# The opening of a feed-forward up stage: sums, casts, a split, a gate and the next stage's first splits issued later; second halves' gates behind the next sums

## The chip, the cores and the metric

The kernel runs on one core of one Trainium2 chip. The metric is device time in microseconds (us) of one execution; a lower time is better. The core's engines work side by side, each on a queue of its own that it works off in order: TensorE (PE, matmuls), VectorE (DVE), ScalarE (ACT), GpSimd (POOL) and SyncE (SP, which here issues the DMAs). PEld is TensorE's weight load.

## The reference, cut to what matters

One decoder layer over 16 + 1024 tokens of width 1024. The first part mixes attention and a recurrence; the change touches its last blocks and what follows, which is the feed-forward part:

```python
h = h + rmsnorm(mix, ln_mix_post[l])
a = rmsnorm(h, ln_ffn_pre[l])
u = a @ w_up                       # 1024 x 5632, D_FF = 2816
u = causal depthwise conv of width 3 over tokens(u) + conv_b
gate, up = split(u, 2)
y = (gelu(gate) * up) @ w_down     # 2816 x 1024
h = h + rmsnorm(y, ln_ffn_post[l])
```

Every matmul is done in float32 accuracy: each operand is split into a rounded high part and a low remainder, and three products (high·high, high·low, low·high) replace one.

## The kernel before, in words

**Blocks.** The first part works in token blocks of 128. Its last step for a block (`post_a`, `post_b`) makes the residual `xh`, then the normalized activations `a2s`; `trans` turns these on TensorE (tile `pa`, L1112) and ACT copies them into `at2_0` or `at2_1`, one tile for each half p of the tokens (p = 0, 1; 512 tokens each). TensorE's order near 650 us is: the last output blocks, `trans(6)`, the first products of the up stage, with `trans(7)` and `trans(8)` between them.

**Up stage.** The 2816 gate columns and the 2816 up columns go in 22 units of 128 + 128 columns, ft = 0 to 21. A unit's weights come by DMA as four raw pieces `ra` (`load_raw4`, on SP, five buffers), GpSimd forms their sums `ws` (`w_sum`), ACT casts the high part `uh`, and DVE or GpSimd subtracts for the low part `ul` (`prep(q)`, q = 7·ft + j). The preparation for unit ft + 1 runs during unit ft.

Units 0 and 1 are `plain_unit`s: for each half, four column pieces of 24 matmuls into banks `pq`, each followed by an ACT copy into `ug` or `uu`. Units 2 to 21 are `unit`s: seven products j = 0 to 6 instead of eight (Winograd's form of Strassen), 12 matmuls each for each half, the halves taking turns. Products 0 and 4 go to bank `pa`, 1, 3 and 5 to `pb`, 2 and 6 to `pc`. Between products the engines read the banks: ACT copies `x1` out of `pa` after product 0; DVE makes `u2` = pb + x1 after product 1, and only then may product 3 write `pb` on; DVE makes `u3` after product 3, and only then product 5 may; then come the halves of `uu` and `ug`. Names end in unit and half: `u2_2_1` is u2 of unit 2, half 1.

The products' token operands are quarters of `at2` and their differences. `t_sums(p)` makes the differences in place (four subtractions of 128 x 1024, `at<-at` in the profile, and a small one for p = 0); `t_split(p, j)` splits a quarter into high (ACT cast) and low (DVE): tiles `t0_j`, `t1_j`. Unit 0 and 1 need j = 0, 4, 7, 6 of the plain quarters, the later units also 1, 2, 3, 5 of the sums.

**Gate.** `gated` takes a unit's `ug` and `uu`: an ACT step and two DVE steps for the convolution of each (tiles `c0` and `c1`), a gelu on ACT, the product on GpSimd (L1280) and a store by SP into `gsc` (L1281). The columns that a second half needs of the first are copied by ACT.

**Down stage.** It reads `gsc` back (`gi`), splits it (`gh` cast on ACT, `gl` on DVE), and multiplies. `ahead(i)` does this for step i, `LOOK` steps before it.

**Who sets the order.** TensorE's order is the written one. For the other engines a scheduler orders the instructions, and `with behind(names)` holds what is issued inside it on an engine's queue behind the instruction last noted in `marks[name]` on that engine; it makes no wait of its own across engines. `issue_after(marks["store"])` does the same on SP for the weight loads: they stand behind the noted store. DVE and ACT instructions go through a recording helper, so that nearly all of them carry line 53 in the profile; tiles tell them apart.

Of the kernel before, what the change touches and what calls it, by code (L numbers as in the profile page):

```python
# [13 lines left out]
ALU = mybir.AluOpType  # L14
# [10 lines left out]
NF = DFF // P  # L25
# [6 lines left out]
HALF = 256  # L32
# [53 lines left out]
def layer_kernel(ctx: ExitStack, tc: tile.TileContext, x, meta, table, lbl, gpre, gpost, win,  # L86
# [63 lines left out]
    def ps_s(name):  # L150
        return pp.tile([P, 2, 512], F32, tag="S", name=name)
# [912 lines left out]
    @contextmanager  # L1064
    def behind(*names):
        with ExitStack() as st:
            for nm in names:
                st.enter_context(tc.issue_after(marks[nm].ins))
            yield
# [68 lines left out]
                      7: (0, e + HALF, e + 2 * HALF), 6: (4, e + HALF, e + 2 * HALF)}[j]  # L1138
        return at2[p][:, k0:k0 + 4, c0:c1]

    def t_sums(p):
        b11, b12, b21, b22 = (quarter(p, j, False) for j in (0, 7, 4, 6))
        V.tensor_tensor(b11, b12, b11, op=ALU.subtract)
        V.tensor_tensor(b12, b22, b12, op=ALU.subtract)
        V.tensor_tensor(b22, b22, b11, op=ALU.subtract)
        V.tensor_tensor(b21, b21, b22, op=ALU.subtract)
        if EDGE[p]:
            e1, e2 = (at2[p][:, k0:k0 + 4, :EDGE[p]] for k0 in (0, 4))
            V.tensor_tensor(e2, e2, e1, op=ALU.subtract)

    def sum_quarter(p, j):
        return {1: lambda: quarter(p, 6), 2: lambda: quarter(p, 0, False), 3: lambda: quarter(p, 7), 5: lambda: quarter(p, 4)}[j]()
# [56 lines left out]
    for n, i in enumerate(order):  # L1209
        py = ps_s(f"py1_{i}")[:, 0]  # L1210
        before = order[n - 1] if n else None
        if i > 2:
            for _ in out_last(i):
                pass
        if i < 2:
            m = (m0, kept)[i]
            todo = [(m[:, 0, a:a + 2], m[:, 1, a:a + 2], a, a + 2, tok(i)[0]) for a in range(0, KD, 2)]
        else:
            todo = ms + [pre_last[i]]
        nxt = []  # L1220
        for c, part in enumerate(todo):
            if c == 2:
                if n == 0:
                    for p in range(3, NBLK):
                        pre_last[p] = mix_split(p, 7, 8)
                else:
                    post_b(before)
                    if n + 1 < NBLK:
                        x_in(order[n + 1])
            if c == 3 and n >= 2:  # L1230
                trans(order[n - 2])
            for _ in out_part(part, py, wo, c == 0, part is todo[-1]):
                pass
            if 1 < i < NBLK - 1 and c < 4:
                nxt.append(mix_load(i + 1, c))
        if i > 1:
            ms = nxt
        if i == 5:
            t_split(0, 0, quarter(0, 0), ep, "e0")
            t_split(0, 4, quarter(0, 4), ep, "e1")  # L1240
        if i == 6:
            t_split(0, 7, quarter(0, 7), mxp, "mix0", 272)
            t_split(0, 6, quarter(0, 6), mxp, "mix1", 384)
        if i == 7:
            t_sums(0)
        if i == 3:
            prep_plain(1, ("12", "22"))
        post_a(i, py)
    post_b(8)
    with behind("rstd"):  # L1250
        prep_plain(1, ("11", "21"))
    close(q_cm, kp_cm, ml_cm, w1_cm, y_cm)

    xu_cm, xup = pool("xu", 2)
# [6 lines left out]

    last = {}

    def conv(ft, p, side, u):
        m = ft + NF * side
        w = 2 * HALF
        if p:
            A.copy(u[:, :2], last[side][:, w:])
        last[side] = u
        c = cv.tile([P, w], F32, tag=f"c{side}", name=f"c{side}_{ft}_{p}", bufs=2 if side else 3)  # L1270
        A.activation(c, u[:, 2:2 + w], AF.Identity, bias=cbt[:, m:m + 1], scale=cwt[:, m, 2:3])
        V.scalar_tensor_tensor(c, u[:, 1:1 + w], cwt[:, m, 1:2], c, ALU.mult, ALU.add)
        V.scalar_tensor_tensor(c, u[:, 0:w], cwt[:, m, 0:1], c, ALU.mult, ALU.add)
        return c

    def gated(ft, p, ug, uu):
        cg = conv(ft, p, 0, ug)
        A.activation(cg, cg, AF.Gelu_apprx_tanh)
        cu = conv(ft, p, 1, uu)
        G.tensor_tensor(cg, cg, cu, op=ALU.mult)  # L1280
        st = SY.dma_start(gsc[P * ft: P * (ft + 1), 2 * HALF * p:2 * HALF * (p + 1)], cg)  # L1281
        if ft == p == 0:
            marks["store"] = st

    def plain_unit(ft, p, bank):
        us = outputs(ft, p)
        e = EDGE[p]
        for col in range(2):
            a, n = ((2 - e, HALF + e), (2 + HALF, HALF))[col]
            for side in range(2):  # L1290
                pt = bank(f"pq{ft}_{p}_{col}{side}")[:, :n]
                for kh in range(2):
                    hi, lo = plain[ft, f"{side + 1}{kh + 1}"]
                    th, tl = tt[p][(0, 4, 7, 6)[2 * col + kh]]
                    for k in range(4):
                        s = slice(P * k, P * (k + 1))
                        T.matmul(pt, hi[:, s], th[:, k], start=(kh + k == 0), stop=False)
                        T.matmul(pt, hi[:, s], tl[:, k], start=False, stop=False)
                        T.matmul(pt, lo[:, s], th[:, k], start=False, stop=(kh == 1 and k == 3))
                A.copy(us[side][:, a:a + n], pt)  # L1300
                yield
        with behind("turned"):
            gated(ft, p, *us)
        yield

    def unit(ft, p, bank):
        nm = f"{ft}_{p}"
        ug, uu = outputs(ft, p)
        e = EDGE[p]
        x1 = xup.tile([P, HALF + 2], F32, tag="x1", name=f"x1_{nm}")[:, 2 - e:]  # L1310
        u2, u3 = (xup.tile([P, HALF], F32, tag=t, name=f"{t}_{nm}") for t in ("u2", "u3"))

        def mm(j, pt, first):
            hi, lo = made[7 * ft + j]
            th, tl = tt[p][j]
            pt = pt[:, HALF + e - width(p, j):]
            for k in range(4):
                s = slice(P * k, P * (k + 1))
                T.matmul(pt, hi[:, s], th[:, k], start=(first and k == 0), stop=False, skip_group_check=True)  # L1319
                T.matmul(pt, hi[:, s], tl[:, k], start=False, stop=False, skip_group_check=True)  # L1320
                T.matmul(pt, lo[:, s], th[:, k], start=False, stop=(k == 3), skip_group_check=True)  # L1321

        pa = bank(f"pa{nm}")[:, :HALF + e]
        mm(0, pa, True)
        A.copy(x1, pa)
        yield
        pb = bank(f"pb{nm}")[:, :HALF + e]
        mm(1, pb, True)
        V.tensor_tensor(u2, pb[:, e:], x1[:, e:], op=ALU.add)
        yield  # L1330
        pc = bank(f"pc{nm}")[:, :HALF + e]
        mm(2, pc, True)
        yield
        mm(3, pb, False)
        V.tensor_tensor(u3, pb[:, e:], x1[:, e:], op=ALU.add)
        V.tensor_tensor(uu[:, 2 + HALF:], pc[:, e:], u3, op=ALU.add)
        yield
        mm(4, pa, False)
        A.copy(ug[:, 2 - e:2 + HALF], pa)
        yield  # L1340
        mm(5, pb, False)
        V.tensor_tensor(uu[:, 2 - e:2 + HALF], pb, x1, op=ALU.add)
        yield
        mm(6, pc, False)
        V.tensor_tensor(ug[:, 2 + HALF:], pc[:, e:], u2, op=ALU.add)
        gated(ft, p, ug, uu)
        yield

    free = [ps_in("pq0"), ps_in("pq1")]
    both = ps_s("pq2")  # L1350
    free += [both[:, 0], both[:, 1]]
    p0 = plain_unit(0, 0, lambda nm: free.pop(0))
    next(p0)
    with behind("xh"):
# [5 lines left out]
        t_split(1, 4, quarter(1, 4), tp, "t1_4")  # L1360
    next(p0)
    trans(8)
    t_split(1, 7, quarter(1, 7), tp, "t1_5")
    t_split(1, 6, quarter(1, 6), mxp, "mix2", 384)
    next(p0)
    with behind("hi", "lo"):
        t_split(0, 1, sum_quarter(0, 1), tp, "t0_1", 264)
        t_split(0, 2, sum_quarter(0, 2), tp, "t0_2")
        t_split(0, 3, sum_quarter(0, 3), tp, "t0_3")
# [8 lines left out]
        next(p1)  # L1378
    prep(14)
    prep(15)  # L1380
    t_sums(1)
    p0 = plain_unit(1, 0, ps_b)
    for j in range(4):
        next(p0)
# [8 lines left out]
    for j in range(4):  # L1393
        next(p1)
    prep(17)
    t_split(1, 5, sum_quarter(1, 5), tp, "t1_5")
    close(a_cms.pop())
    dn_cm, dn = pool("down", 4, "right")
    for j in range(4, 7):
        prep(14 + j)  # L1400
    next(p1)
    for ft in range(2, NF):
        units = [unit(ft, p, ps_b) for p in range(2)]
        for j in range(7):
            prep(7 * (ft + 1) + j)
            for u in units:
                next(u)
    close(t2_cm, t_cm, v_cm, xu_cm, mx_cm)

    f_cm, fp = pool("fin", 1)  # L1410
# [171 lines left out]
            SY.dma_start(out[P * (4 + m): P * (5 + m), :], hh4[:, m])  # L1582

    LOOK = 3
    for i in range(LOOK):
        ahead(i)
    for i, (pr, k) in enumerate(steps):
        ahead(i + LOOK)
        if k == 0:
            banks[pr] = banks[5] if pr == 3 else banks[6] if pr == 7 else [ps_b(f"pd{pr}_{m}") for m in range(5 if pr == 4 else 4)]  # L1590
            if pr == 5:
# [98 lines left out]
```

## Time and profile before

| what | us |
|---|---|
| median of 3 runs | 1337.39 |
| lowest and highest of these | 1335.03, 1341.37 |
| the profiled execution, its own time | 1337.54 |
| its span, first to last instruction | 1335.8 |
| up stage's units 2 to 21, from about | 705 |
| PE waits shown from 640 to 820 (total) | 11.9 |

The span is what the trace covers; the execution's own time has 1.7 us more around it. The mean granted clock of TensorE in the span was 0.995. In the profile's rows names stand without their numbers, `c<-ug,cwt,c` is a convolution step of a gate's c0 tile, `c<-uu,cwt,c` one of c1, `t<-at,t` the low part of a token split, `u<-pb,x` is u2 or u3, and the bracket at the end of a row is the idle time of the engine just before it and what ended it.

### The profile page before, as it was taken

To read this page: it belongs to the slowest core of one execution; us is meant where nothing else is said; L and a number is where in the kernel's file an instruction comes from. 1 tells how busy PE (TensorE), PEld (TensorE's weight loads), DVE (VectorE), ACT (ScalarE), POOL (GpSimd) and SP (SyncE) were. 2 spreads that over 40 slices of the span, in tenths; PEclk is the share of its full clock that TensorE was granted. 3 is DMA by queue.
4 is the path that set the end of the run, shared out by engine and by line. 5 is a ranking of instruction groups with operands and counts; after the bars stand their busy time and mean duration, and the time that the engine had idled before them with its cause. 6 is when DMAs were issued, how large, how long until landed. Compare 5 with 4: busy or idle time off the path is not lost. (4 is left out here: it accounts for less than half of the span.)

```text
span 1335.8 us, 26319 instructions
## 1 busy us (share of the span) xinstructions
PE 1288.8 (96%) x10227; PEld 1191.1 (89%) x10227; DVE 914.6 (68%) x1589; ACT 690.3 (52%) x1670; POOL 414.1 (31%) x324
## 2 busy tenths in 40 slices
PE   6999999999999999999898999999999999999997
PEld 5898899989999999777798999999999998888886
DVE  7666657564756465836788787877777776697587
ACT  7365356534654565446655454454454454454454
POOL 3211211121202110122157566666657641010021
PEclk9999999999999999999998999999999999999999
DMA  6331333132311112826512222223222225964363
GB/s 215 108 125 60 104 101 122 52 128 92 115 36 34 32 33 66 259 96 231 187 64 88 95 73 82 84 76 115 80 82 78 80 80 177 330 218 154 107 205 119
DMA packets 84371, 153.07 MB, mean 115 GB/s; under 512 B 9571, under 2 KB 19843, under 8 KB 84246
## 3 DMA queue, kind: packets, MB, share of 16 engines
q1 hardware_dynamic: 84246, 151.39, 34.1%
q8 instruction: 80, 1.31, 0.4%
q14 instruction: 45, 0.37, 0.1%
HBM read 112.69 MB, written 38.67 MB: 113 GB/s over the span
## 5 line engine op out<-in xcount | busy, mean ns | idle before, releaser
L1319 PE MATMUL pb<-t,uh 128*128 128x258 f32 (+1 forms) x480 | 136.9, 285 | 8.1 <-DVE u L53 8.1
L1320 PE MATMUL pb<-t,uh 128*128 128x258 f32 (+1 forms) x480 | 135.6, 283 | 0.0
L1321 PE MATMUL pb<-t,ul 128*128 128x258 f32 (+1 forms) x480 | 135.6, 283 | 0.0
L1503 PE MATMUL pd<-wl,gh 128*128 128x512 f32 (+1 forms) x314 | 122.2, 389 | 0.3 <-DVE wl L53 0.2
L1504 PE MATMUL pd<-wh,gl 128*128 128x512 f32 (+1 forms) x314 | 122.1, 389 | 0.0
L1502 PE MATMUL pd<-wh,gh 128*128 128x512 f32 (+1 forms) x314 | 122.0, 388 | 0.0
L53 DVE SCALAR_TENSOR_TENSOR c<-uu,cwt,c 128x512 f32<-128x512 f32 x88 | 94.9, 1079 | 20.2 <-ACT c L53 19.5
L1280 POOL TENSOR_TENSOR c<-c,c 128x512 f32<-128x512 f32 x44 | 66.9, 1520 | 132.0 <-ACT c L53 123.6
L1319 PEld LDWEIGHTS pb<-t,uh 128*128 128x128 f32 x480 | 91.6, 191 | 9.2 <-DVE u L53 8.9
L1321 PEld LDWEIGHTS pb<-t,ul 128*128 128x128 f32 x480 | 92.0, 192 | 0.0
L1320 PEld LDWEIGHTS pb<-t,uh 128*128 128x128 f32 x480 | 91.4, 190 | 0.0
L1319 PE MATMUL pa<-t,uh 128*128 128x258 f32 (+1 forms) x320 | 90.2, 282 | 0.0
L1320 PE MATMUL pa<-t,uh 128*128 128x258 f32 (+1 forms) x320 | 89.9, 281 | 0.0
L1321 PE MATMUL pc<-t,ul 128*128 128x256 f32 x320 | 89.9, 281 | 0.0
L1319 PE MATMUL pc<-t,uh 128*128 128x256 f32 x320 | 89.9, 281 | 0.0
L1320 PE MATMUL pc<-t,uh 128*128 128x256 f32 x320 | 89.9, 281 | 0.0
L1321 PE MATMUL pa<-t,ul 128*128 128x258 f32 (+1 forms) x320 | 89.7, 280 | 0.0
L53 DVE SCALAR_TENSOR_TENSOR c<-ug,cwt,c 128x512 f32<-128x512 f32 x88 | 86.4, 982 | 1.8 <-ACT c L53 1.1
L1503 PEld LDWEIGHTS pd<-wl,gh 128*128 128x128 f32 x314 | 59.2, 189 | 13.9 <-DVE wl L53 1.0
L1504 PEld LDWEIGHTS pd<-wh,gl 128*128 128x128 f32 x314 | 59.3, 189 | 12.8
L1502 PEld LDWEIGHTS pd<-wh,gh 128*128 128x128 f32 x314 | 59.3, 189 | 12.8
L155 POOL TENSOR_TENSOR ul<-ws,uh 128x512 fp32r<-128x512 f32 x40 | 58.2, 1454 | 35.4 <-ACT uh L53 31.6
(411 smaller groups left out, 4205.2 us busy)
## 6 DMA issues: line engine op xcount, KB each, us to landing
ra<-in_wup_dram SPq DMA_DIRECT2D x80, 256.0 KB, 2.7
wd<-in_wdown_dram SPq DMA_DIRECT2D x44, 256.0 KB, 4.6
tsc<-wd SPq DMA_DIRECT2D x44, 256.0 KB, 2.9
gsc<-c SPq DMA_DIRECT2D x44, 256.0 KB, 2.0
wi<-tsc SPq DMA_DIRECT2D x44, 256.0 KB, 2.8
gi<-gsc SPq DMA_DIRECT2D x33, 256.0 KB, 3.6
wi<-in_wdown_dram SPq DMA_DIRECT2D x33, 256.0 KB, 3.4
msc<-mm SPq DMA_DIRECT2D x21, 256.0 KB, 3.5
```

The source lines that it names most:

```text
L53: ins = call(*args, **kw)
L155: (eng or G).tensor_tensor(lo, raw, hi.bitcast(F32), op=ALU.subtract)
L1280: G.tensor_tensor(cg, cg, cu, op=ALU.mult)
L1319: T.matmul(pt, hi[:, s], th[:, k], start=(first and k == 0), stop=False, skip_group_check=True)
L1320: T.matmul(pt, hi[:, s], tl[:, k], start=False, stop=False, skip_group_check=True)
L1321: T.matmul(pt, lo[:, s], th[:, k], start=False, stop=(k == 3), skip_group_check=True)
L1502: T.matmul(py, gh[:, s], wh, start=(k == 0 and pr not in (3, 7)), stop=False, skip_group_check=True)
L1503: T.matmul(py, gh[:, s], wl, start=False, stop=False, skip_group_check=True)
L1504: T.matmul(py, gl[:, s], wh, start=False, stop=(k == NH - 1), skip_group_check=True)
```

## The change

It changes the order of work around the start of the up stage, in seven places; the matmuls are the same and in the same order.

1. `t_sums(0)` is cut in two: two subtractions behind `xh` of block 7, the rest among the splits for unit 2.
2. The banks `pq2` and `pq3` of the first plain unit become tiles of their own, instead of two parts of one.
3. The casts for two pieces of unit 1's weights (`prep_plain(1, ("11", "21"))`) come later, behind the turning of block 8.
4. `marks["store"]` is set by the store of (1,0) too, and not by that of (0,0) alone. Loads asked for after it stand behind it on SP.
5. The gates of second halves (p = 1, from unit 1 on) are kept in `waiting` and issued behind `u2` of the next unit; the copies for the seam are taken out of `conv` and stay in place.
6. In unit 2 the preparation of j = 0 and 1 of unit 3 and the split `t1_5` are issued behind `u2` too.
7. The down stage's `ahead(0)` to `ahead(3)` are issued behind `u2` and `x1` of unit 19.

```diff
-    def t_sums(p):
+    def t_sums(p, part):
         b11, b12, b21, b22 = (quarter(p, j, False) for j in (0, 7, 4, 6))
-        V.tensor_tensor(b11, b12, b11, op=ALU.subtract)
-        V.tensor_tensor(b12, b22, b12, op=ALU.subtract)
+        if part == 0:
+            V.tensor_tensor(b11, b12, b11, op=ALU.subtract)
+            V.tensor_tensor(b12, b22, b12, op=ALU.subtract)
+            return
...
-        if i == 7:
-            t_sums(0)
+        if i == 8:
+            with behind("xh"):
+                t_sums(0, 0)
...
-    with behind("rstd"):
-        prep_plain(1, ("11", "21"))
...
-        if ft == p == 0:
+        if ft < 2 and p == 0:
             marks["store"] = st
+
+    waiting = []
+
+    def gate_waiting():
+        with behind("u2"):
+            while waiting:
+                gated(*waiting.pop(0))
...
-        gated(ft, p, ug, uu)
+        seam(p, (ug, uu))
+        if p:
+            waiting.append((ft, p, ug, uu))
+        else:
+            gated(ft, p, ug, uu)
...
-    both = ps_s("pq2")
-    free += [both[:, 0], both[:, 1]]
+    free += [ps_s(f"pq{n}")[:, 0] for n in (2, 3)]
...
     trans(8)
+    with behind("turned"):
+        prep_plain(1, ("11", "21"))
...
     with behind("hi", "lo"):
+        t_sums(0, 1)
...
-    t_split(1, 5, sum_quarter(1, 5), tp, "t1_5")
-    close(a_cms.pop())
-    dn_cm, dn = pool("down", 4, "right")
...
         for j in range(7):
-            prep(7 * (ft + 1) + j)
+            if ft > 2 or j > 1:
+                prep(7 * (ft + 1) + j)
             for u in units:
                 next(u)
+            if j == 1:
+                if ft == 2:
+                    with behind("u2"):
+                        prep(21)
+                        prep(22)
+                        t_split(1, 5, sum_quarter(1, 5), tp, "t1_5")
+                    close(a_cms.pop())
+                    dn_cm, dn = pool("down", 4, "right")
+                gate_waiting()
+        if ft == NF - 3:
+            marks["u2 late"], marks["x1 late"] = marks["u2"], marks["x1"]
+    gate_waiting()
...
-    for i in range(LOOK):
-        ahead(i)
+    with behind("u2 late", "x1 late"):
+        for i in range(LOOK + 1):
+            ahead(i)
     for i, (pr, k) in enumerate(steps):
-        ahead(i + LOOK)
+        if i:
+            ahead(i + LOOK)
```

DVE around block 6's `a2s`, which `trans(6)` turns; `at2_0` are the subtractions of `t_sums(0)`. Before:

```order
L53 TENSOR_TENSOR y0_6299<-y0_6299,pz7_7635 128x512
L53 TENSOR_TENSOR at2_0_7158<-at2_0_7158 128x4x256 x2
L53 TENSOR_TENSOR y0_6299<-y0_6299,pz8_7707 128x512
L53 TENSOR_TENSOR at2_0_7158<-at2_0_7158 128x4x256
L53 SCALAR_TENSOR_TENSOR a2s_7261<-xh6_7518,ssy_6301,gfb_7164 128x1024
L53 TENSOR_TENSOR tmp7_7699<-py1_7_7634,gpo_7162 128x512
```

The same place now:

```order
L53 TENSOR_TENSOR y0_6299<-y0_6299,pz8_7702 128x512
L53 TENSOR_TENSOR tmp7_7694<-py1_7_7634,gpo_7162 128x512
L53 SCALAR_TENSOR_TENSOR a2s_7261<-xh6_7518,ssy_6301,gfb_7164 128x1024
L53 SCALAR_TENSOR_TENSOR xh7_7591<-y0_6299,ssy_6301,xh7_7591 128x512
L53 SCALAR_TENSOR_TENSOR xh7_7591<-tmp7_7694,ssy_6301,xh7_7591 128x512
L53 TENSOR_TENSOR at2_0_7158<-at2_0_7158 128x4x256 x2
```

The three subtractions moved from ahead of `a2s` to behind it, two of them behind `xh7`.

SP from the first store of the up stage on; `gsc` rows are stores of gates (unit and half in the name behind the arrow), `ra3` rows loads of unit 3's weights. Before:

```order
L1281 DMA gsc_92<-c0_0_0_7936 128x512
L1159 DMA ra2_11_8083<-in_wup_dram 128x512
L1159 DMA ra2_22_8085<-in_wup_dram 128x512
L1159 DMA ra2_21_8087<-in_wup_dram 128x512
L1159 DMA ra2_12_8089<-in_wup_dram 128x512
L1159 DMA ra3_11_8390<-in_wup_dram 128x512
L1159 DMA ra3_22_8392<-in_wup_dram 128x512
L1159 DMA ra3_21_8394<-in_wup_dram 128x512
L1281 DMA gsc_92<-c0_0_1_8069 128x512
L1281 DMA gsc_92<-c0_1_0_8231 128x512
L1159 DMA ra3_12_8396<-in_wup_dram 128x512
```

The same place now:

```order
L1285 DMA gsc_92<-c0_0_0_7934 128x512
L1161 DMA ra2_11_8084<-in_wup_dram 128x512
L1161 DMA ra2_22_8086<-in_wup_dram 128x512
L1161 DMA ra2_21_8088<-in_wup_dram 128x512
L1161 DMA ra2_12_8090<-in_wup_dram 128x512
L1285 DMA gsc_92<-c0_0_1_8071 128x512
L1285 DMA gsc_92<-c0_1_0_8232 128x512
L1161 DMA ra3_11_8439<-in_wup_dram 128x512
L1161 DMA ra3_22_8441<-in_wup_dram 128x512
L1161 DMA ra3_21_8443<-in_wup_dram 128x512
L1161 DMA ra3_12_8445<-in_wup_dram 128x512
```

Three loads of unit 3's weights moved behind two stores.

DVE in unit 2, from the last low part of unit 2's weights to `u3_2_0`. Before:

```order
L53 TENSOR_TENSOR ul19_8366<-ra2_22_8085,uh19_8365 128x512
L53 SCALAR_TENSOR_TENSOR c0_1_1_8376<-ug1_1_8242,cwt_88,c0_1_1_8376 128x512 x2
L53 TENSOR_TENSOR t1_5_8354<-at2_1_7154,t1_5_8354 128x1024
L53 SCALAR_TENSOR_TENSOR c1_1_1_8382<-uu1_1_8243,cwt_88,c1_1_1_8382 128x512
L53 TENSOR_TENSOR ul21_8389<-ra3_11_8390,uh21_8388 128x512
L53 SCALAR_TENSOR_TENSOR c1_1_1_8382<-uu1_1_8243,cwt_88,c1_1_1_8382 128x512
L53 TENSOR_TENSOR ul22_8441<-ws2_8442,uh22_8440 128x512
L53 TENSOR_TENSOR u2_2_0_8405<-pb2_0_8446,x1_2_0_8404 128x256
L53 TENSOR_TENSOR gl1_0_13697<-gi1_0_13692,gh1_0_13696 128x512
L53 TENSOR_TENSOR u2_2_1_8424<-pb2_1_8460,x1_2_1_8423 128x256
L53 TENSOR_TENSOR gl1_1_13709<-gi1_1_13704,gh1_1_13708 128x512
L53 TENSOR_TENSOR ul24_8505<-ws3_8506,uh24_8504 128x512
```

The same place now:

```order
L53 TENSOR_TENSOR ul19_8360<-ra2_22_8086,uh19_8359 128x512
L53 TENSOR_TENSOR u2_2_0_8374<-pb2_0_8409,x1_2_0_8373 128x256
L53 TENSOR_TENSOR u2_2_1_8393<-pb2_1_8423,x1_2_1_8392 128x256
L53 TENSOR_TENSOR ul21_8438<-ra3_11_8439,uh21_8437 128x512
L53 TENSOR_TENSOR ul22_8452<-ws2_8453,uh22_8451 128x512
L53 TENSOR_TENSOR t1_5_8457<-at2_1_7154,t1_5_8457 128x1024
L53 SCALAR_TENSOR_TENSOR c0_1_1_8464<-ug1_1_8243,cwt_88,c0_1_1_8464 128x512
L53 SCALAR_TENSOR_TENSOR c1_1_1_8469<-uu1_1_8244,cwt_88,c1_1_1_8469 128x512
L53 SCALAR_TENSOR_TENSOR c0_1_1_8464<-ug1_1_8243,cwt_88,c0_1_1_8464 128x512
L53 SCALAR_TENSOR_TENSOR c1_1_1_8469<-uu1_1_8244,cwt_88,c1_1_1_8469 128x512
L53 TENSOR_TENSOR ul24_8506<-ws3_8507,uh24_8505 128x512
L53 TENSOR_TENSOR u3_2_0_8375<-pb2_0_8409,x1_2_0_8373 128x256
```

The pair of u2 moved ahead of the four convolution steps of gate (1,1), of t1_5, ul21 and ul22, which now stand between u2 and u3; the subtractions gl1 are gone from here. On ACT the cast `uh21` stands ahead of the copy `x1_2_0`, and the cast `uh22` ahead of `x1_2_1`, in both kernels.

More of the change, by code (lines that the diff above doesn't have):

```diff
@@ L1262, in layer_kernel, with seam @@
     last = {}
+    def seam(p, us):
+        for side in range(2):
+            if p:
+                A.copy(us[side][:, :2], last[side][:, 2 * HALF:])
+            last[side] = us[side]
     def conv(ft, p, side, u):
@@ L1266, in conv @@
         w = 2 * HALF
-        if p:
-            A.copy(u[:, :2], last[side][:, w:])
-        last[side] = u
         c = cv.tile([P, w], F32, tag=f"c{side}", name=f"c{side}_{ft}_{p}", bufs=2 if side else 3)
@@ L1301, in plain_unit @@
                 yield
-        with behind("turned"):
-            gated(ft, p, *us)
+        seam(p, us)
+        if ft and p:
+            waiting.append((ft, p, *us))
+        else:
+            with behind("turned"):
+                gated(ft, p, *us)
         yield
@@ L1324, in unit @@
         mm(0, pa, True)
-        A.copy(x1, pa)
+        marks["x1"] = A.copy(x1, pa)
         yield
@@ L1328, in unit @@
         mm(1, pb, True)
-        V.tensor_tensor(u2, pb[:, e:], x1[:, e:], op=ALU.add)
+        marks["u2"] = V.tensor_tensor(u2, pb[:, e:], x1[:, e:], op=ALU.add)
         yield
@@ L1345, in unit @@
         V.tensor_tensor(ug[:, 2 + HALF:], pc[:, e:], u2, op=ALU.add)
-        gated(ft, p, ug, uu)
+        seam(p, (ug, uu))
+        if p:
+            waiting.append((ft, p, ug, uu))
+        else:
+            gated(ft, p, ug, uu)
         yield
     free = [ps_in("pq0"), ps_in("pq1")]
-    both = ps_s("pq2")
-    free += [both[:, 0], both[:, 1]]
+    free += [ps_s(f"pq{n}")[:, 0] for n in (2, 3)]
     p0 = plain_unit(0, 0, lambda nm: free.pop(0))
@@ L1362, in layer_kernel @@
     trans(8)
+    with behind("turned"):
+        prep_plain(1, ("11", "21"))
     t_split(1, 7, quarter(1, 7), tp, "t1_5")
@@ L1380, in layer_kernel @@
     prep(15)
-    t_sums(1)
+    t_sums(1, 0)
+    t_sums(1, 1)
     p0 = plain_unit(1, 0, ps_b)
```

## The prediction

> **What bounds the kernel now.** I read the page's head first, then the chain and the waits of TensorE by stretches, then the windows around the longest wait, then single instructions there.
>
> ```profile
> span 1335.8 us, 26319 instructions
> PE 1288.8 (96%) x10227; PEld 1191.1 (89%) x10227; DVE 914.6 (68%) x1589; ACT 690.3 (52%) x1670; POOL 414.1 (31%) x324
> ```
>
> TensorE (PE) is busy for 96% of the span, and its matmuls and their order are the same in both kernels, so the change can only win or lose time in which PE waits or runs at a lower clock. The waits of PE from 640 to 820 us, as engine, tile and line waited for, total us, times and longest:
>
> ```profile
> PE pa L1112 <- DVE a2s L53: 2.4, 1, 2.4
> PE pq L1297 <- ACT ug L53: 1.4, 1, 1.4
> PE pb L1319 <- DVE u L53: 6.3, 1, 6.3
> PE pb L1319 <- DVE u L53: 1.8, 3, 0.7
> ```
>
> The windows (us, then busy us and count of PE, PEld, DVE, ACT, POOL, then granted clock, DMA share, GB/s) say where nothing can be won:
>
> ```profile
> 640.00:700.00 60.00, 56.18 (x424) 52.97 (x423) 48.44 (x45) 36.96 (x81) 21.17 (x11) 1.00 0.35 120
> 715.00:720.00 5.00, 0.00 (x0) 0.00 (x0) 4.71 (x7) 4.14 (x9) 0.67 (x1) 0.78 0.63 197
> 720.00:725.00 5.00, 4.82 (x24) 4.82 (x25) 5.00 (x6) 0.94 (x2) 4.84 (x4) 0.54 0.25 93
> 800.00:1100.00 300.00, 300.00 (x2540) 299.81 (x2539) 229.04 (x334) 148.42 (x288) 188.88 (x133) 1.00 0.25 84
> ```
>
> From 800 us on PE never waits. Around 720 us it stands still, and after the wait the clock is 0.54. PE's own rows give the cost:
>
> ```profile
> 654.59 1.09 PE L1112 MATMUL pa<-ident,a2s 128*128 128x128 f32 x8 [2.37 <-DVE a2s L53]
> 667.87 0.38 PE L1297 MATMUL pq<-t,uh 128*128 128x256 f32 x1 [1.38 <-ACT ug L53]
> 705.22 0.29 PE L1319 MATMUL pa<-t,uh 128*128 128x258 f32 x1
> 720.18 0.58 PE L1319 MATMUL pb<-t,uh 128*128 128x256 f32 x1 [6.31 <-DVE u L53]
> 733.63 0.28 PE L1319 MATMUL pa<-t,uh 128*128 128x258 f32 x1
> 753.52 0.29 PE L1319 MATMUL pa<-t,uh 128*128 128x258 f32 x1
> ```
>
> Unit 2 (705.22 to 733.63) takes 28.41 us, unit 3 takes 19.89. So unit 2 loses 8.5 us: 6.31 of wait and 2.2 of lower clock. With 2.37, 1.38 and the three small waits (1.8), the stake is 14.1 us, 1.05% of the time.
>
> **Part 1: sums behind block 7, own banks, later casts.** The DVE rows ahead of the 2.37 us wait:
>
> ```profile
> 647.15 3.46 DVE L53 TENSOR_TENSOR at<-at 128x1024 f32<-128x1024 f32 x2
> 651.12 1.21 DVE L53 TENSOR_TENSOR at<-at 128x1024 f32<-128x1024 f32 x1
> 652.26 2.28 DVE L53 SCALAR_TENSOR_TENSOR a2s<-xh,ssy,gfb 128x1024 f32<-128x1024 f32 x1
> ```
>
> Three subtractions, 4.7 us, stand ahead of a2s and now stand behind it; only tmp (0.7 us) comes in front instead. Up to 4 us earlier is more than 2.37, so I count 2.3 for that wait. The pq wait goes because the banks are no longer one tile: 1.4. What comes later: the third subtraction stands among the splits for unit 2, 45 us before use; the casts of uh1 (ACT) stand in front of two casts and the first gate, for which I charge 1.1 us below. Their bound is 0 to 1.4, the second figure if PE meets a late ug copy anyhow. PE is thus 3.7 us early from 668 us on, and unit 2 starts at 705.2 − 3.7 = 701.5.
>
> **Part 2: the weight loads behind two more stores.** This is where I expect the gain to be lost. Rows of SP, ACT and POOL around the first store:
>
> ```profile
> 679.96 4.21 POOL L1280 TENSOR_TENSOR c<-c,c 128x512 f32<-128x512 f32 x1 [10.26 <-ACT c L53]
> 684.57 12.06 SPq L1159 DMA_DIRECT2D ra<-in_wup_dram  x7
> 688.00 0.62 ACT L53 CAST uh<-ra 128x512 fp32r<-128x512 f32 x1 [5.52 <-DMA ra<-in_wup_dram]
> 689.86 1.81 POOL L1163 TENSOR_TENSOR ws<-ra,ra 128x512 f32<-128x512 f32 x1 [5.69 <-DMA ra<-in_wup_dram]
> 691.75 2.16 POOL L1163 TENSOR_TENSOR ws<-ws,ra 128x512 f32<-128x512 f32 x1
> 706.14 2.14 POOL L1280 TENSOR_TENSOR c<-c,c 128x512 f32<-128x512 f32 x1 [1.48 <-ACT ug L53]
> ```
>
> Before, seven loads, those of unit 3's first three pieces among them, start right behind the first store. Now those wait for the store of (1,0), that is for the product at 706.14 to 708.28. From the first product's end (684.17) to that point lie 24.1 us of DVE and POOL work, which the change does not shorten. The first product moves 3.7 earlier with PE and 1.1 later with the casts, and a shorter overlap with DVE may save part of its 4.21 us (other products take 2.14): I take its end at 680 (678.7 to 683.4), and the second store's at T = 680 + 24 = 704 (702 to 707).
>
> Then the chain seen above repeats for unit 3's weights: cast of uh21 3.8 us after T, first weight sum 5.7 after T, two sums of 1.3 to 2.2, cast of uh22 (0.6), copy x1 and u2 (0.4 each). In ACT's order uh21 stands ahead of x1_2_0 and uh22 ahead of x1_2_1, so u2_2_0 comes at 704 + 5.3 = 709.3 and u2_2_1 at 704 + 10.4 = 714.4. PE needs u2_2_0 in front of product 3: 720.18 − 6.31 − 705.22 = 8.65 us after unit 2's start, at 710.2; and u2_2_1 one half product (19.89/14 = 1.42) later, at 711.6. First half in time, second half 2.8 us late.
>
> **Part 3: the gate behind u2.** DVE in unit 2 before:
>
> ```profile
> 713.23 2.55 DVE L53 SCALAR_TENSOR_TENSOR c<-ug,cwt,c 128x512 f32<-128x512 f32 x2
> 715.69 1.22 DVE L53 TENSOR_TENSOR t<-at,t 128x1024 fp32r<-128x1024 f32 x1
> 717.18 0.75 DVE L53 SCALAR_TENSOR_TENSOR c<-uu,cwt,c 128x512 f32<-128x512 f32 x1 [0.27 <-ACT c L53]
> 717.85 0.68 DVE L53 TENSOR_TENSOR ul<-ra,uh 128x512 fp32r<-128x512 f32 x1
> 719.71 0.42 DVE L53 TENSOR_TENSOR u<-pb,x 128x256 f32<-128x256 f32 x1
> 720.05 1.43 DVE L53 TENSOR_TENSOR gl<-gi,gh 128x512 fp32r<-128x512 f32 x1
> 723.10 1.76 DVE L53 TENSOR_TENSOR ul<-ws,uh 128x512 fp32r<-128x512 f32 x1
> 724.78 0.41 DVE L53 TENSOR_TENSOR u<-pb,x 128x256 f32<-128x256 f32 x1
> ```
>
> Four convolution steps, the split t1_5, ul21 and ul22 stood ahead of u2_2_0 and cost the 6.3 us; now they stand between u2_2_1 and u3_2_0, with ul24. That is eight instructions: alone 4 × 0.75 + 1.22 + 3 × 0.68 = 6.3 us, beside POOL at the longer figures (2.55 for two, 1.76, and 2.3 for an operation of 1024) 4 × 1.28 + 2.3 + 3 × 1.76 = 12.7. POOL works half of this stretch, making unit 3's sums, so I take 9: u3_2_0 ends at 714.4 + 9 + 0.4 = 723.8. PE needs it for product 5, four half products behind product 3's first half: 710.2 + 5.7 + 2.8 = 718.7. It waits 5.1 us. What queues behind u3 on DVE is uu, which frees no bank sooner than needed.
>
> The clock: the wait of 2.37 us left it at 1.00 (window 640 to 700), the one of 6.31 cost 2.2. For 5.1 I take 1.0, bounds 0 and 2.2. [...]
>
> Unit 2 then loses 2.8 + 5.1 + 1.0 = 8.9 us against 8.5. Ends: with T at 702 and DVE alone, 0.4 + 2.3 = 2.7; with T at 707 and DVE crowded, 16.
>
> **Part 4: later units.** Each gate of a second half now stands behind u2. The tightest point before was a steady unit's u2:
>
> ```profile
> 919.28 2.45 DVE L53 SCALAR_TENSOR_TENSOR c<-ug,cwt,c 128x512 f32<-128x512 f32 x2
> 922.26 0.74 DVE L53 TENSOR_TENSOR u<-pb,x 128x256 f32<-128x256 f32 x2
> 924.05 1.52 DVE L53 TENSOR_TENSOR ul<-ws,uh 128x512 fp32r<-128x512 f32 x1 [1.05 <-ACT uh L53]
> 923.26 0.28 PE L1319 MATMUL pb<-t,uh 128*128 128x256 f32 x1
> ```
>
> u2's pair ended at 923.0, 0.3 us ahead of its matmul. The three small waits in units 3 to 5 (1.8 us) are this margin missed, and they go. The new tight point is u3: u2's second half is possible 4 half products (5.7 us) into the unit, done at 6.1; four steps at 1.28 and ul at 1.52 bring 12.7, u3 13.1; PE needs it at 14.2 (10 half products). Margin 1.1: cost 0.
>
> **Part 5: the down stage's first splits.** Eight operations (four casts, four subtractions) leave units 2 to 5, where two of the subtractions (the row at 720.05 is one) stood next to u2, and come into unit 19, two of the subtractions ahead of its u3. They take 1.4 to 2.9 us there against that margin of 1.1: late by 0.3 to 1.8, I take 0.8. Their loads stay early; four other loads move to units 18 and 19 in SP's queue, where SP waits for nothing that PE needs within a unit: 0.
>
> **The sum**, against the profiled execution: 2.3 + 1.4 + (8.5 − 8.9) + 1.8 − 0.8 = 4.3 us gained. That execution took 1337.54 us (span 1335.8 and 1.7 around it), 0.15 above the median of 1337.39. So 1333.1.
>
> **Rivals.** (a) The stall goes: T comes at 702, POOL is out of DVE's way, unit 2 loses 2.7: 2.3 + 1.4 + 5.8 + 1.8 = 11.3 gained, 1326. For it speaks that the first product's 4.21 us is unlike the others; against it that the load chain alone is 10.4 us. Chance of ending between 1326 and 1330.7: 0.27. (b) My forecast, the stall is moved and not removed, 1331 to 1336: 0.49. (c) It grows: T at 706 to 707, unit 2 loses 13 to 16, which eats parts 1 and 4: 1337 to 1341: 0.13, mostly still near no change. (d) Slower: u3 becomes late in every unit. If the four steps run at the 1.78 us that a contended step took at its worst,
>
> ```profile
> 692.68 1.78 DVE L53 SCALAR_TENSOR_TENSOR c<-uu,cwt,c 128x512 f32<-128x512 f32 x1
> ```
>
> u3 comes at 6.1 + 7.1 + 1.5 + 0.4 = 15.1, 0.9 late in each of 19 units: 17 us, 1350. It decides from 1.6 us per step on; the steady rows, with 1.2 on the average, speak against it. 0.08. (e) PE's early gain in part 1 does not arise, since another writer holds the bank or a2s is late for xh: 1337: 0.03.
>
> **The numbers.** A measurement of this kernel tells about 0.5%, 6.7 us, from no change. Faster by more (below 1330.7): (a), 0.27 and a little of (b), 0.28. Slower (above 1344): (d) and the end of (c), 0.09. The rest 0.63. The range 1326 to 1340 runs from (a)'s best to most of (c). (b)'s own is 1331 to 1336.
>
> **What would show it.** No wait of pa (L1112) on a2s, none of pq on ug; unit 2 starting near 701.5; the first load of ra3 behind the store at 704 and not behind the one at 680; x1_2_1 waiting on ACT behind uh22; two waits of pb on u in unit 2, 2.8 and 5.1 us, with one stretch of lower clock; no wait from unit 3 to 18; one under 2 us in unit 19. I am wrong if unit 2 takes under 24 us (the load chain is hidden), or if waits on u recur in every unit.

## The result, and the profile after

The change makes the kernel slower: 1351.59 us (median of 5 runs, 1349.70 to 1354.01) against 1339.85 us (5 runs of the kernel before, 1335.03 to 1341.50), ratio 1.0101, 95% interval 1.0077 to 1.0126. The two kernels' runs do not overlap, so a loss of 1% is clear of their spread. The forecast was 1333.1, a small gain. The profiled execution took 1351.59 us with a span of 1349.8, 14.0 more than before. All further comparisons of stretches are made between the profiled executions.

The head of the page after:

```profile
span 1349.8 us, 26304 instructions
PE 1291.3 (96%) x10227; PEld 1191.0 (88%) x10227; DVE 934.7 (69%) x1589; ACT 684.3 (51%) x1670; POOL 416.1 (31%) x324
```

The waits of TensorE after, in the stretches 700 to 720, 720 to 760, 760 to 820 and 820 to 1090 us (engine, tile, line, releaser, total us, times, longest); from 640 to 700 there is none:

```profile
PE pb L1334 <- DVE u L53: 2.9, 2, 2.4
PE pb L1334 <- DVE u L53: 5.9, 2, 5.6
PE pb L1334 <- DVE u L53: 2.4, 3, 0.9
PE pb L1334 <- DVE u L53: 12.1, 13, 2.1
```

The last row is new: the stretch that had no wait at all before now has one in every unit. The window there and that of the two waits that did go:

```profile
640.00:700.00 60.00, 59.91 (x465) 57.34 (x464) 51.17 (x47) 38.34 (x83) 18.46 (x11) 1.00 0.31 106
...
800.00:1100.00 300.00, 287.01 (x2396) 283.89 (x2395) 238.11 (x319) 135.03 (x272) 186.68 (x129) 0.99 0.24 79
```

PE is busy for 59.9 of the 60 us up to 700, 3.7 more than before, and for 287.0 instead of 300.0 us between 800 and 1100. PE's own rows:

```profile
700.24 0.29 PE L1334 MATMUL pa<-t,uh 128*128 128x258 f32 x1
709.42 0.39 PE L1334 MATMUL pb<-t,uh 128*128 128x256 f32 x1 [0.53 <-DVE u L53]
713.47 0.38 PE L1334 MATMUL pb<-t,uh 128*128 128x256 f32 x1 [2.40 <-DVE u L53]
723.60 0.58 PE L1334 MATMUL pb<-t,uh 128*128 128x258 f32 x1 [5.58 <-DVE u L53]
933.01 0.39 PE L1334 MATMUL pb<-t,uh 128*128 128x258 f32 x1 [0.87 <-DVE u L53]
953.87 0.39 PE L1334 MATMUL pb<-t,uh 128*128 128x258 f32 x1 [0.86 <-DVE u L53]
1080.39 0.39 PE L1334 MATMUL pb<-t,uh 128*128 128x258 f32 x1 [2.10 <-DVE u L53]
```

These are waits of products 3 (128x256) and 5 (128x258), that is for u2 and u3. Two neighbouring waits on u3 lie 953.87 − 933.01 = 20.86 us apart: a unit takes 20.86, not 19.85. Where the 14.0 us come from, by the first matmul of each unit (from PE's rows of both kernels):

| stretch | before | after | difference |
|---|---|---|---|
| start of unit 2 | 705.22 | 700.24 | −5.0 |
| unit 2 | 28.41 | 30.33 | +1.9 |
| units 3 to 5 | 61.96 | 62.08 | +0.1 |
| units 6 to 18 (13 units) | 258.3 | 271.3 | +13.0 |
| unit 19 | 19.85 | 23.83 | +4.0 |

Of the 5.0 us at unit 2's start 0.75 lies ahead of the edited stretch, where the two executions differ: block 5 is turned at 644.99 before and at 644.24 after. From there to unit 2 TensorE takes 60.23 and 56.00 us; 3.75 of these 4.2 us are the two waits that went.

The cause of the 13 us can be read off the chain of waits. Between 921 and 958 us it runs over VectorE and ScalarE alone (start, us, engine, tile, line; rows under 0.4 us are left out):

```profile
921.54 0.76 DVE c L53
...
942.40 0.76 DVE c L53
943.19 0.63 ACT c L53
944.08 0.53 ACT uh L53
944.63 1.11 DVE ul L53
945.74 0.66 DVE u L53 x2
946.41 4.45 DVE c L53 x3
950.90 0.51 issue
951.41 0.61 ACT uh L53
952.05 1.43 DVE ul L53
953.85 0.44 DVE uu L53
955.35 0.53 ACT uh L53
955.90 1.09 DVE ul L53
957.43 0.82 ACT c L53
```

It comes back to the same step 942.40 − 921.54 = 20.86 us later. So the order of the two queues has closed into a loop of its own: u2, the held conv steps, their gelu (the 0.51 "issue" at 950.90 is that, ACT's row below), the cast and low part of the next unit's product 3 weights, u3 and uu, the next cast and low part, this unit's first gate, its gelu, the cast behind that, the low part, and u2 of the next unit. TensorE hands over in between, but the chain has no TensorE step here: the loop sets the pace. VectorE's idle times of over 0.5 us from 938.67 to 959.5 all end with ScalarE, and ScalarE's all with VectorE. VectorE there, row by row, with the ScalarE instruction that it waits for:

```profile
945.66 0.74 DVE L53 TENSOR_TENSOR u<-pb,x 128x256 f32<-128x256 f32 x2
946.33 1.12 DVE L53 SCALAR_TENSOR_TENSOR c<-ug,cwt,c 128x512 f32<-128x512 f32 x1
947.37 1.77 DVE L53 SCALAR_TENSOR_TENSOR c<-uu,cwt,c 128x512 f32<-128x512 f32 x1
949.07 1.77 DVE L53 SCALAR_TENSOR_TENSOR c<-ug,cwt,c 128x512 f32<-128x512 f32 x1
950.77 0.74 DVE L53 SCALAR_TENSOR_TENSOR c<-uu,cwt,c 128x512 f32<-128x512 f32 x1
952.05 1.43 DVE L53 TENSOR_TENSOR ul<-ws,uh 128x512 fp32r<-128x512 f32 x1 [0.55 <-ACT uh L53]
953.40 0.41 DVE L53 TENSOR_TENSOR u<-pb,x 128x256 f32<-128x256 f32 x1
```

```profile
950.88 0.63 ACT L53 ACTIVATE c<-c 128x512 f32<-128x512 f32 x1 [5.76 <-DVE c L53]
951.41 0.60 ACT L53 CAST uh<-ws 128x512 fp32r<-128x512 f32 x1
```

u3 ends at 953.81 and the matmul starts at 953.87. ScalarE had stood idle for 5.76 us ahead of the gelu, and the cast that VectorE needs next was queued behind it.

### The profile page after: what moved, and what is told of

Read it like the earlier page. It is cut to its first block, busy times and chain, and to the rows that moved or that the text cites. A ratio compares the mean times of both kernels' runs of the same rounds, so it can differ in the third digit from the quotient of the medians.

```text
span 1349.8 us, 26304 instructions
## 1 busy us (share of the span) xinstructions
PE 1291.3 (96%) x10227; PEld 1191.0 (88%) x10227; DVE 934.7 (69%) x1589; ACT 684.3 (51%) x1670; POOL 416.1 (31%) x324
## 4 chain that ended last, share of the span: by engine, by line
PE 45%; DVE 23%; ACT 10%; issue 6%; DMA 4%; SPq 0%; POOL 0%; ACTq 0%; DVEq 0%; POOLq 0%
DVE c L53 9%; DVE ul L53 5%; PE pd L1535 5%; PE pd L1536 5%; PE pd L1534 5%; ACT c L53 3%; ACT uh L53 2%; PE pa L708 2%; PE py L969 2%; PE py L973 1%; DMA wd<-in_wdown_dram 1%; PE py L971 1%; DVE uu L53 1%; DVE u L53 1%; PE pi_hi L231 1%
## 5 line engine op out<-in xcount | busy, mean ns | idle before, releaser
L53 DVE SCALAR_TENSOR_TENSOR c<-uu,cwt,c 128x512 f32<-128x512 f32 x88 | 100.8, 1146 | 19.5 <-ACT c L53 19.5
L53 DVE SCALAR_TENSOR_TENSOR c<-ug,cwt,c 128x512 f32<-128x512 f32 x88 | 92.7, 1053 | 11.5 <-ACT c L53 11.5
L1284 POOL TENSOR_TENSOR c<-c,c 128x512 f32<-128x512 f32 x44 | 60.6, 1377 | 113.1 <-ACT c L53 100.7
L53 ACT ACTIVATE c<-c 128x512 f32<-128x512 f32 x44 | 27.8, 632 | 125.2 <-DVE c L53 125.2
L53 DVE TENSOR_TENSOR ul<-ws,uh 128x512 fp32r<-128x512 f32 x40 | 49.4, 1235 | 35.8 <-ACT uh L53 35.8
```

The costliest lines, as they stand in the source:

```text
L53: ins = call(*args, **kw)
```

## Experiments

Theory: the loop, made by the gates behind u2 (edit 5). The rivals, each as it stands in the expectations: another edit; the gelu ahead of the cast; GpSimd's contention. The first four kernels shared 19 runs of the kernel before (median 1338.03 us).

**gates_in_place: edit 5 undone for units 2 to 21.**

```diff
         seam(p, (ug, uu))
-        if p:
+        if False:
             waiting.append((ft, p, ug, uu))
```

> The changed kernel, but from unit 2 on the gates of second halves are issued where they were before; the gate of (1,1) still waits for u2 of unit 2, all else stays changed. Theory (closed chain): with the gates behind u2 a unit's work on VectorE and ScalarE closes into a chain of 20.86 us, longer than TensorE's 19.85, so u3 is late by 0.9 in every unit; with the gates back the 13 waits of 0.74 to 0.89 between 820 and 1060 us go and units take 19.85 again: about 1337 (the opening's early gain of 3.8, unit 2's loss and the three small waits of units 3 to 5 back). Rival (the loss comes from another edit, the later weight loads or the down stage's splits): units stay at 20.86 and the time at 1349 to 1352.

1336.94 us, ratio to the kernel before 0.9989 (0.9975 to 1.0003). The window:

```profile
820.00:1060.00 240.00, 240.00 (x2031) 239.80 (x2031) 183.76 (x266) 119.53 (x232) 154.96 (x109) 1.00 0.24 81
```

PE is busy throughout, units 3 to 18 take 19.84 to 19.95. Units 3 to 5 sum to 59.65, 2.3 less than before: the down stage's splits are gone from there, and in no_down below, where they are back, units 3 to 5 are long again. Unit 2 takes 30.89 and unit 19 23.44: these losses belong to other edits.

**only_gates: the kernel before with edit 5 alone, from unit 2 on.** `seam`, `waiting` and `gate_waiting` as in the change; the gate of (1,1), the loads and the splits stay.

> The kernel before, with one edit alone: gates of second halves from unit 2 on behind u2 of the next unit. Theory (closed chain): each unit from 3 on takes 1.0 us longer, 18 of them, the three small waits of units 3 to 5 are part of it: 1354 to 1357. Rival (the loss needs the other edits too): within 3 us of the kernel before.

1352.95 us, ratio 1.0106 (1.0089 to 1.0123). The one edit reproduces the whole loss:

```profile
820.00:1060.00 240.00, 231.08 (x1938) 228.86 (x1938) 188.72 (x253) 107.44 (x217) 150.58 (x104) 1.00 0.24 81
```

Units 6 to 19 take 20.72 to 20.99. Its time is a little under the range given, since units 3 to 5 were not at 19.85 before and unit 20 stays at 19.84. With gates_in_place this shows that edit 5 is the cause of the 13 us.

**cast_first: the held gate's gelu behind the cast for product 3's weights, from unit 3 on.**

```diff
+    def gelu_late():
+        while late:
+            ft, p, cg, cu = late.pop(0)
+            with behind("hi4"):            # the cast of prep's j == 3
+                A.activation(cg, cg, AF.Gelu_apprx_tanh)
+            product(ft, p, cg, cu)
```

> The changed kernel, but from unit 3 on the gelu of the waiting gate stands behind ScalarE's cast for product 3's weights instead of ahead of it. Theory (closed chain on both engines): the gelu's 0.63 us leave the chain between the conv steps and u3, the wait at u3 falls from 0.87 to about 0.2 a unit: 1340 to 1343. Rival A (the gelu ahead of the cast is the whole cause): no wait, 1338. Rival B (VectorE's queue alone is the cause, the cast is not waited for): no change, 1351.

1340.79 us, ratio 1.0022 (1.0011 to 1.0033). The waits of PE between 820 and 1060 us, and VectorE behind the conv steps:

```profile
PE pb L1353 <- DVE u L53: 1.5, 8, 0.2
```

```profile
942.91 0.74 DVE L53 SCALAR_TENSOR_TENSOR c<-uu,cwt,c 128x512 f32<-128x512 f32 x1
943.58 0.68 DVE L53 TENSOR_TENSOR ul<-ws,uh 128x512 fp32r<-128x512 f32 x1
944.18 0.41 DVE L53 TENSOR_TENSOR u<-pb,x 128x256 f32<-128x256 f32 x1
```

ul follows the last step at once and takes 0.68 instead of 1.43, and u3 comes 1.27 us behind the last step's start instead of 2.63. Two things changed for ul: it no longer waits for the cast, and it starts ahead of GpSimd's product of the held gate (943.79), beside which it ran before (951.64). Units 7 to 18 take 20.0 to 20.3, and of the 13.0 us of units 6 to 18 3.4 are left; unit 19 takes 24.35, a little more than in the change. So the position of one cast against the gelu on ScalarE carries most of the loss, and the four steps on VectorE leave a wait of up to 0.2 us: the loop goes over both engines, as the theory had it, and neither queue alone is the cause.

**no_sums: GpSimd's four weight sums left out from unit 4's weights on.**

```diff
-            w_sum("1", raws["21"], raws["22"], ALU.add)
+            w_sum("1", raws["21"], raws["22"], ALU.add, ft > 3)   # returns its first operand
```

> The changed kernel, but GpSimd's four weight sums are left out from unit 4's weights on (the raw pieces are used in their place), so the products are not the reference's; everything else keeps its place. Rival C (the order alone makes u3 late, contention with GpSimd adds nothing): the waits stay at 0.8 to 0.9 a unit, 1350. Theory (the conv steps at 1.77 us beside GpSimd are what makes the chain longer than TensorE's unit): the steps fall to 0.75, the chain by 2 us, no waits from unit 4 on: about 1337.

1332.37 us, ratio 0.9945 (0.9925 to 0.9966). With the gates still behind u2, the window is full again:

```profile
820.00:1060.00 240.00, 240.00 (x2034) 240.00 (x2033) 180.98 (x266) 118.58 (x233) 83.22 (x61) 1.00 0.25 81
```

Of the four steps one takes 1.77, beside GpSimd's low part at 958.07, and three 0.74 (from 957.94 us on: 0.73, 1.77, 0.74, 0.74). The cast still stands behind the gelu and is still waited for (0.54 us), but u3 ends 12.5 us into the unit (964.11 − 951.63). Every unit from 3 on takes 19.84 or 19.85, unit 19 too. The order makes the loop, GpSimd's work beside it makes the loop longer than TensorE's unit. The time is below what I gave since unit 19's loss goes as well.

**part1: the kernel before with edits 1 to 3 alone.**

> The kernel before with the first three edits alone: the sums of half 0 cut in two, own banks for pq2 and pq3, the casts for unit 1's weights later. Theory (the early gain is real and independent): no wait on a2s and none on ug from 640 to 700 us, 3.7 us less in this stretch; unit 2 still waits on u2 by some 6 to 10 us, since what stands ahead of it on VectorE does not move with TensorE: 1334 to 1338 against 1338. Rival (TensorE's gain is lost whole at unit 2, which waits for VectorE and GpSimd): unit 2's loss grows from 8.5 to 12 and the time is unchanged within 1 us.

1336.81 us, ratio 0.9987 (0.9976 to 0.9998), this time and the next three against 27 runs of the kernel before (median 1337.73). From 640 to 700 us PE is busy for 59.90 us, so the early 3.7 us are real; from block 5's turn to unit 2 TensorE takes 55.98 us, 4.2 less than before. But:

```profile
721.89 0.58 PE L1320 MATMUL pb<-t,uh 128*128 128x256 f32 x1 [8.58 <-DVE u L53]
```

The wait in unit 2 grows from 6.31 to 8.58 and the unit from 28.41 to 31.19: 2.8 of the 4.2 us are given back. Counted from block 5's turn (648.40 here, 644.99 before), the matmul that waits for u2 starts only 1.7 us earlier: VectorE's work ahead of u2 does not come as much earlier as TensorE does. The truth lies between theory and rival, nearer to the rival.

**no_store: the change with edit 4 undone** (`if ft == p == 0` again). One execution, 1347.59 us, so only its rows are read here.

> The changed kernel, but the mark on the store is set by the first store alone, as before, so unit 3's weight loads are not behind two more stores. Theory (load chain): the copy x1 of unit 2's second half no longer stands behind a cast whose weights are late; the wait of 2.4 us at 713 (u2_2_1) goes. The longer one (5.6 us, u3 behind eight instructions) stays or grows by as much as u2 comes earlier on TensorE only, 3 to 8 us: unit 2 takes 28 to 30 instead of 30.3. Rival (the copy waits for something else): both waits stay.

Unit 2 takes 28.43 instead of 30.33:

```profile
712.81 0.58 PE L1334 MATMUL pb<-t,uh 128*128 128x256 f32 x1 [2.33 <-DVE u L53]
722.74 0.42 PE L1334 MATMUL pb<-t,uh 128*128 128x258 f32 x1 [2.53 <-DVE u L53]
```

The wait of the second half for u2 (2.40) is gone as expected. In the changed kernel the copy x1 of that half stood on ScalarE behind a cast that waited for a weight sum:

```profile
712.07 0.62 ACT L53 CAST uh<-ws 128x512 fp32r<-128x512 f32 x1 [3.16 <-POOL ws L1165]
712.60 0.37 ACT L53 COPY x<-pa 128x256 f32<-128x256 f32 x1
```

Here the cast has no wait ahead of it. But the first half now waits 2.33, for VectorE's own work. The later wait is halved: counted from the unit's start (700.24 and 701.50), VectorE comes to u3 2.1 us earlier, and TensorE comes to it 0.9 later, after a stretch at clock 0.50 behind the wait of 2.33. Over unit 2 the waits fall by 3.5 us, and the clock takes 1.6 of it back, for two such stretches stand here against one in the change. So the later loads cost unit 2 1.9 us in these two executions; best against down_spread below, with two such stretches in each, gives 2.0.

**no_down: gates_in_place with edit 7 undone as well.**

> The kernel with gates of units 2 to 21 in place (gates_in_place), and also the down stage's first splits issued where they were before (units 2 to 5). Theory: the 3.6 us that unit 19 takes above 19.85 there (a wait of 1.9 on u3 and half clock behind it) are the price of these splits: unit 19 takes 19.85, and units 2 to 5 get back at most the 1.8 us of small waits: 2 to 3.6 us less than gates_in_place. Rival (unit 19 is long for the gate or the loads of the down stage): unit 19 stays at 23.4.

1338.19 us, ratio 1.0001 (0.9988 to 1.0013). Unit 19 takes 19.94, so its 3.6 us are the price of the splits there. But unit 2 takes 31.87 and unit 3 23.63, where VectorE stands for 4.5 us behind a split whose input is not there:

```profile
745.94 1.29 DVE L53 TENSOR_TENSOR gl<-gi,gh 128x512 fp32r<-128x512 f32 x1 [4.50 <-ACT gh L53]
```

My "at most 1.8 us" for units 2 to 5 missed this. The split reads back the gate of unit 2's first half, and its load is issued on SP at 741.34, right behind the stores of unit 2's gates (from 738.34). In the kernel before it stood there too, at 743.03, and VectorE waited 1.86 us for it; why the wait is longer here is open.

**opening_u3: gates of units 2 to 21 in place, edit 7 undone, and in unit 2 the held work behind u3.**

```diff
-                        prep(21)
-                        prep(22)
                         t_split(1, 5, sum_quarter(1, 5), tp, "t1_5")
...
+            if ft == 2 and j == 3:
+                gate_waiting()                 # now behind("u3")
+                with behind("uu", "x1"):
+                    for q in range(21, 25):
+                        prep(q)
```

> The changed kernel with three things redone: gates of units 2 to 21 in place; the down stage's splits where they were before; and in unit 2 the gate of (1,1) behind u3 instead of u2, the preparation of unit 3's first four weights behind that and behind the copies x1 on ScalarE; t1_5 stays behind u2. Theory (the opening is a matter of what stands ahead of u2 and u3): unit 2's loss falls from 10.5 to 0 to 3 us, the early 3.7 us stay: 1324 to 1329 against 1338 of the kernel before. Rival (VectorE has too much work in this stretch, wherever it stands): the wait moves to uu2_1, ahead of product 6, or to unit 3's start, and unit 2 and 3 together still lose 6 to 10: 1332 to 1336.

1340.85 us, ratio 1.0028 (1.0019 to 1.0037): worse than both theory and rival gave, and the rival is nearer. Unit 2 takes 27.86 and unit 3 28.83.

```profile
719.61 0.69 DVE L53 TENSOR_TENSOR gl<-gi,gh 128x512 fp32r<-128x512 f32 x1 [7.72 <-ACT gh L53]
```

A late split stands in VectorE's queue again, here the first one, ahead of uu, u3 of the second half and the gate. It costs 7.7 us of idle time: VectorE is there at 711.9, and the split's load is issued at 715.72, behind six weight loads (from 704.37). What was held is then done in unit 3. This run doesn't tell how the held work would do without that split.

**down_spread: gates_in_place, and the four splits one each in units 18 to 21.** This run and the next share 9 runs of the kernel before (median 1338.58).

```diff
-    with behind("u2 late", "x1 late"):
-        for i in range(LOOK + 1):
+    for i in range(LOOK + 1):
+        with behind(f"uu {NF - 4 + i}", f"x1 {NF - 4 + i}"):
             ahead(i)
```

> The kernel with gates of units 2 to 21 in place (gates_in_place), but the down stage's four splits are issued one each in units 18 to 21, behind that unit's uu (VectorE) and x1 (ScalarE), where VectorE stood idle for 2.5 us in every unit. Theory (four subtractions in one place ahead of u3 cost unit 19 its 3.6 us): units 18 to 21 take 19.85 each, 3.6 us less than gates_in_place, 1333 to 1335. Rival (they cost wherever they stand, or their inputs come late): 2 or more us lost over units 18 to 21, 1335 to 1338.

1332.64 us, ratio 0.9956 (0.9939 to 0.9973), a little under the range. Units 18 to 20 take 19.85, 19.84 and 19.85. The splits cost nothing in VectorE's idle time behind uu.

**best: down_spread with edit 4 undone.**

> As down_spread, and the mark on the store set by the first store alone, as in the kernel before. Theory: unit 2 falls from 30.9 to about 28.4 as it did in no_store, all units from 3 on at 19.85: 1331 to 1333 against 1338 of the kernel before. Rival (the earlier loads set GpSimd's sums beside VectorE's work ahead of unit 2, and u2 comes as much later): unit 2 and the start of unit 2 together gain less than 1 us over down_spread.

1330.06 us, ratio 0.9942 (0.9928 to 0.9957), a little under the range and the fastest order of this study. All of its up stage's waits on u from 640 to 1110 us:

```profile
PE pb L1334 <- DVE u L53: 4.9, 2, 2.7
```

Unit 2 takes 28.56 (30.53 in down_spread), all units from 3 on 19.84 to 20.00. So in the profiled execution 4.0 us are won up to unit 2 (from block 5's turn) and 2.4 in units 3 to 5, and nothing in unit 2, which took 28.41 before. What is left of the stake is unit 2, 8.7 us: 4.9 in the two waits, and nearly all the rest in a stretch of lower clock behind each (the falls at 710.83 and 721.07).

## Why the prediction was wrong

**Part 4 failed, and it decided the sign.** Without it (gates_in_place, 0.9989 with an interval of 0.9975 to 1.0003) the change can't be told from no change. It set the new tight point's cost at 0 by a margin of 1.1 us at u3. Its start was mis-sized: "u2's second half is possible 4 half products (5.7 us) into the unit, done at 6.1". u2 stands behind the low part of the weights and the first half's gate on VectorE, and in the row that the prediction itself quotes, the pair ended at 923.0 with the unit begun at 914.77: 8.2 us into the unit. After the change it ends 946.40 − 938.67 = 7.7 us in. The four steps took 5.1 us as forecast (946.40 to 951.51), ul 1.43 against 1.52, but a wait of 0.55 us for the cast behind the gelu was not in the sum at all; I had not looked at where the held gate's gelu falls on ScalarE, nor followed the two queues round to the next unit. 1.6 later at the start and 0.55 for the cast, less 0.1 on ul, put u3 at 15.1 us into the unit instead of 13.1: a margin of 1.1 became a wait of 0.9. The prediction's own sign of being wrong, waits on u in every unit, is what came. Rival (d) named this result with 0.9 us a unit and got a chance of 0.08; its mechanism (steps all at 1.78) was not the one, two of the four took 1.77, so that it came to the same 15.1 is luck. The three small waits of units 3 to 5 were replaced and not won.

**Part 5 was right in kind and too small.** 0.8 was forecast at unit 19; against a unit of 20.86 it takes 3.0 more. The wait is 2.10 instead of 0.9, and a stretch of half clock follows it, 1.7, for which the forecast had no term.

**Part 1 held as a wait, not wholly as a gain.** Both waits went, 3.75 us against 3.7. With these edits alone (part1) 2.8 us come back in unit 2, since VectorE, for which unit 2 waits, gains less than TensorE. The sum counts the 3.7 in full; in the whole change unit 2 is 1.9 longer than before, against 0.4 forecast.

**Parts 2 and 3 were close.** Unit 2's waits are 0.53, 2.40 and 5.58 against 0, 2.8 and 5.1, the clock 2.0 against 1.0: 10.5 against 8.9. In this execution one stretch of lower clock fell into unit 2; in down_spread, with 7.0 us of waits there, it was two. T, the second store, was forecast for 704; the store's product ran from 701.78 to 703.93. That is in part luck: the first product ended at 677.92 and not at 680, and from there it took 26.0 us and not 24.1. That the load chain sets the 2.40 is read from the cast's row under no_store; why unit 2 still loses 8.7 us in the best order is open: it waits for VectorE's own work ahead of u2, and opening_u3, which was to move it, failed for another reason.

The sum by the profile: −4.2 (up to unit 2) −0.75 (ahead of the stretch) + 1.9 + 0.1 + 13.0 + 4.0 = 14.05 against a forecast of −4.3.

## What to carry to other kernels

When instructions are held behind a point that repeats in a loop, follow the whole cycle on every engine's queue, back to the same instruction one round later: if its length is near the bound engine's round (here 20.86 us against 19.85), the new order may set the pace by itself, and every round pays. Take the start of such a walk from a row of the trace and not from when the input could be ready at the earliest. And time won ahead of a wait for another engine is won only if that engine's work also moves: in part1 2.8 of 4.2 us came back.

## What the runs showed of the hardware

**Some short waits were followed by half the clock, depending on where they fell.** The wait of 2.10 us that ended at 1080.39 was followed by a lower clock, in windows of the kernel after:

```profile
1080.00:1082.00 2.00, 1.61 (x12) 1.61 (x12) 2.00 (x5) 0.00 (x0) 2.00 (x2) 0.89 0.72 227
1082.00:1084.00 2.00, 2.00 (x9) 1.71 (x9) 2.00 (x5) 1.26 (x4) 0.83 (x1) 0.50 0.58 176
1084.00:1086.00 2.00, 2.00 (x16) 2.00 (x15) 1.06 (x3) 1.25 (x2) 0.00 (x0) 0.76 0.85 265
```

Here the clock falls about 1.2 us after PE is busy again and stays at 0.50 for about 3.4 us. A wait of 1.89 us in unit 19 of gates_in_place and one of 1.91 in unit 3 of no_down cost 1.7 and 1.9 us in the same way, while the wait of 2.40 at 713 us in the kernel after left the clock at 1.00. The same wait of product 3 lasted 2.38 us in down_spread (to 717.38) and 2.38 in no_sums (to 717.03). Here are the same four microseconds of both, down_spread first:

```profile
717.00:721.00 4.00, 3.62 (x19) 3.62 (x20) 4.00 (x4) 1.00 (x2) 3.84 (x4) 0.61 0.19 50
717.00:721.00 4.00, 3.97 (x34) 3.97 (x35) 4.00 (x3) 0.67 (x2) 3.92 (x3) 1.00 0.28 81
```

The traces show more when their windows are laid on the falls of the clock. Two falls of one trace, read from windows of 0.1 us, lie a whole number of 3.413 us apart in best (710.83 and 721.07, 10.24 us, 3 times) and in the kernel after (723.17 and 1081.56, 358.39 us, 105 times). Counted in such steps from 640 to 1105 us in all twelve traces, every step at full clock in which PE was idle for 1.89 us or more in all was followed by one at 0.50, and none with 1.86 or less was. The 2.40 of the kernel after is divided by such a boundary at 712.93 into 1.86 and 0.54, the 2.38 of no_sums at 715.88 into 1.23 and 1.15; the 2.38 of down_spread lies in one step. This is read from runs made for other questions; none was made to test it.

**VectorE beside GpSimd.** A conv step took 0.74 us alone and 1.77 beside a weight sum of GpSimd (1.62 to 1.63), and leaving the sums out (no_sums) turned two such steps into one. The price is 1.03 us a step (1.77 − 0.74), less than the whole sum; the step at 947.37 began 0.40 us into a sum, with 1.23 of it left.
